# Stick-breaking attention without weights: running products applied to differences of neighbouring values, and wide weight splits moved to VectorE

## The chip, the cores and the metric

The kernel runs on one core of a Trainium2 chip. The metric is the device time of one execution in microseconds (us), as the median of several runs. The engines are named as the profile names them: PE is TensorE (PEld its weight loads), DVE is VectorE, ACT is ScalarE, POOL is GpSimd, and SP is SyncE, which issues the DMAs.

## What is computed

Two decoder layers over 1024 tokens of width 1024, all in float32. Each layer projects x with w_in, runs three token mixers side by side (4 heads of stick-breaking attention, 4 of latent attention with a softmax, called MLA, and 8 of RWKV-7), applies w_o and a layer norm, then a gated feed-forward network with a second layer norm. The part that is changed is stick-breaking attention, per block of 128 queries:

```python
z = jnp.einsum('bhqd,bhkd->bhqk', qb, k).astype(jnp.float32) * scale
past = kpos[None, :] < qpos[:, None]
log_keep = jnp.where(past, jax.nn.log_sigmoid(-z), 0.0)
log_later = lax.cumsum(log_keep, axis=3, reverse=True) - log_keep
w = jnp.where(past, jnp.exp(jax.nn.log_sigmoid(z) + log_later), 0.0)
return jnp.einsum('bhqk,bhkd->bhqd', w.astype(v.dtype), v)
```

With keep = sigmoid(-z), a key's weight is (1 - keep) times the product of the keeps of all later keys. So the weight of key j is R(j+1) - R(j), where R(j) is the running product of the keeps from j to the end.

## The kernel before

One layer is written as four stages: phase A (the projections, the preparation of RWKV, its triangular inverse `rw_inv` and its recurrent chain), attention (MLA and stick-breaking interleaved), the output projection, and the feed-forward network. In the first layer phase A lies at about 20 to 545 us of the profile, attention at 545 to 737, and the feed-forward network runs to 1555. The second layer repeats this.

Every matrix product works on a float32 operand split in two, hi and lo, with three products per tile. `split` (lines 197 to 199) makes them: ScalarE casts hi, and then another engine subtracts it from the source to get lo. For a weight tile of 128x1024 that engine is an argument: VectorE, or GpSimd where `eng` says so. `wload` (line 230) loads a weight tile by one SyncE DMA into `raw` and splits it into `whi` and `wlo`, two buffers each. GpSimd takes the subtraction in `proj_sb`, in `proj_rw` for the feature tiles 1 to 3 of phase A, and for four of the eight tiles of w_o (`w0l`, and `wol` with k of 2 and 5). That is 38 splits in the two layers: 30 of `wlo`, four of `w0l` and four of `wol`.

Attention runs as two generators per mixer (`hp` 0 and 1, for the two heads of a pair), and each yields a block of queries at a time. A stick block (`stick_block`, `stick_post`) takes a score tile from PE, applies tanh(z/2) on ScalarE into `mexp` (three buffers), masks the diagonal square with an affine select on GpSimd (line 393), and then runs three steps on VectorE: keep = 0.5 - 0.5 tanh of the keys shifted by one into `kp`, one of the three buffers LA, T and pd (line 394); the running product from the end (line 396); and the weight, (1 + tanh) times the running product (line 397). PE transposes the weights (`w_transpose`, line 336), ScalarE copies them out, and once both heads of the pair are there `av_store` multiplies them with V. Blocks of pair 0 go from 1 to 8 tiles of keys, blocks of pair 1 from 8 to 1, so there are 64 stick blocks in the two layers.

Where each instruction stands in its engine's queue is decided by the framework's scheduler from its own estimates and the priorities in `PRIORITY`; every engine then runs its queue strictly in that order. A change in one instruction's engine can therefore move others.

Of the kernel before, what the change touches and what calls it, by code (L numbers as in the profile page):

```python
# [12 lines left out]
ALU = mybir.AluOpType  # L13
# [4 lines left out]
P = 128  # L18
S = 1024
# [3 lines left out]
NT = S // P  # L23
IN_COLS = 2912
SBQ, SBK, SBV = 0, 256, 512
# [44 lines left out]
class Body:  # L70
    def __init__(self, ctx, tc, a):
        self.ctx, self.tc, self.nc, self.a = ctx, tc, tc.nc, a
        self.n = 0
        self.ptags = {}
        self.rot = 0
        self.sq = 0
        self.sn = self.kn = 0
        self.pairs = {}

    def nm(self, s):  # L80
# [180 lines left out]
    def proj_sb(self, l, pool, step):  # L261
        nc, W = self.nc, self.a["w_in"][l]
        for j in range(2):
            for base, dst in ((SBQ, self.sqd), (SBK, self.skd)):
                hi, lo = self.wload(W, [(base + j * P, P)], nc.gpsimd)
                d = self.t(pool, [P, S], "pst", bufs=4)
                self.proj_copy(hi, lo, d)
                nc.sync.dma_start(dst[j], d)
                step(4)
        for j in range(2):  # L270
            hi, lo = self.wload(W, [(SBV + j * P, P)], nc.gpsimd)
            d = self.t(pool, [P, S], "pst", bufs=4)
            self.proj_copy(hi, lo, d)
            o = self.t(pool, [P, S], "pst", bufs=4)
            for q in range(2):
                pt = self.ps2()
                for i in range(4):
                    ii = 4 * q + i
                    nc.tensor.transpose(pt[:, i * P : i * P + P], d[:, ii * P : ii * P + P], self.ident)
                nc.vector.tensor_copy(o[:, q * 512 : q * 512 + 512], pt)  # L280
            step(4)
            nc.sync.dma_start(self.svd[j], o.rearrange("p (i v) -> p i v", v=P))
# [29 lines left out]
        for a, b in zip(ms, ms[1:]):  # L312
            self.tc.add_manual_dep(b.ins, a.ins.name, mybir.DependencyInfo(mybir.DependencyClass.NoSync, mybir.DependencyReason.DATA), reason="array halves take turns")

    def attn_out(self, wts, nb, V, av):
        ms = []
        for j in range(nb):
            for hp in range(2):
                hc = slice(hp * 64, hp * 64 + 64)
                ms.append(self.nc.tensor.matmul(av[hc], V[:, j, hc], wts[hp][:, j, :], start=j == 0, stop=j == nb - 1))  # L320
        self.in_order(ms)

    def pieces(self, LL):
# [16 lines left out]
    def stick(self, wp, ip, hp):  # L340
        for pr in range(2):
            if hp == 0:
                self.sv = self.t(wp, [P, NT, P], "mv")
                self.nc.sync.dma_start(self.sv, self.svd[pr])
            V = self.sv
            qk = self.stick_qk(wp, pr, hp)
            for i in range(NT)[:: 1 - 2 * pr]:
                self.stick_block(i, pr, hp, qk, V, wp, ip)
                yield

    def stick_qk(self, wp, pr, hp):
        nc = self.nc
# [19 lines left out]
    def stick_block(self, i, pr, hp, qk, V, wp, ip):  # L372
        nc = self.nc
        mm = nc.tensor.matmul
        q2, k2, kl = qk
        nb, LL = i + 1, (i + 1) * P
        qs = slice(i * P, i * P + P)
        be = self.t(wp, [P, S], "mexp", bufs=3)
        n = self.sn = self.sn + 1
        self.kn += 1  # L380
        kp = self.kp3[self.kn % 3]
        for u, (a0, a1) in enumerate(self.pieces(LL)):
            self.sq = 1 - self.sq
            s = self.pst(("py", "pq")[self.sq])[:, : a1 - a0]
            mm(s, q2[:, qs], k2[:, a0:a1], start=True, stop=False)
            mm(s, q2[:, qs], kl[:, a0:a1], start=False, stop=True)
            nc.scalar.activation(be[:, a0:a1], s, AF.Tanh, scale=0.0625)
        self.stick_post(be, kp, i, LL, nb, n, V, hp, pr, wp)

    def stick_post(self, be, kp, i, LL, nb, n, V, hp, pr, wp):  # L390
        nc = self.nc
        dg = be[:, i * P : LL]
        nc.gpsimd.affine_select(out=dg, in_=dg, pattern=[[-1, P]], base=0, channel_multiplier=1, compare_op=ALU.is_gt, fill=-1.0)  # L393
        nc.vector.tensor_scalar(kp[:, : LL - 1], be[:, 1:LL], -0.5, 0.5, op0=ALU.mult, op1=ALU.add)
        kv = kp[:, : LL - 1][:, ::-1]
        nc.vector.tensor_tensor_scan(kv, kv, self.ones.to_broadcast([P, LL - 1]), 1.0, op0=ALU.mult, op1=ALU.mult)
        nc.vector.scalar_tensor_tensor(be[:, :LL], be[:, :LL], 1.0, kp[:, :LL], op0=ALU.add, op1=ALU.mult)  # L397
        wt = self.w_transpose(self.wt4[:, n % 6], be, nb, "pa")
        self.pair(("s", pr, i), wt, hp, nb, V, self.mixd[pr], i, wp, "pa", 0.5)

    def pair(self, key, wt, hp, *args):
        if key in self.pairs:
# [4 lines left out]
            self.pairs[key] = wt  # L407

    @prioritized
    def av_store(self, wts, nb, V, dst, i, wp, tag, sc):  # L410
        nc = self.nc
        av = self.pst(tag)[:, :P]
        self.attn_out(wts, nb, V, av)
        ot = self.t(wp, [P, P], "avo", bufs=2)
        nc.scalar.mul(ot, av, sc)
        nc.sync.dma_start(dst[:, i * P : i * P + P], ot)

    def exact2(self, ps, st, src, tp, rows=slice(0, P)):
# [146 lines left out]
    def mla_post(self, st, e, pcs, n, nb, sc, pr, hp, i, V, wp):  # L565
        nc = self.nc
        if n == 1:
            nc.vector.reciprocal(st[:, 6:7], st[:, 4:5])
        else:
            nc.scalar.activation(st[:, 7:8], st[:, 0:1], AF.Exp, scale=sc, bias=st[:, 3:4])  # L570
            nc.vector.scalar_tensor_tensor(st[:, 5:6], st[:, 4:5], st[:, 7:8], st[:, 5:6], op0=ALU.mult, op1=ALU.add)
            nc.vector.reciprocal(st[:, 6:7], st[:, 5:6])
        for u, (a0, a1) in enumerate(pcs):
            if u < n - 1:
                nc.vector.tensor_scalar(e[:, a0:a1], e[:, a0:a1], st[:, 7:8], st[:, 6:7], op0=ALU.mult, op1=ALU.mult)
            else:
                nc.vector.tensor_scalar(e[:, a0:a1], e[:, a0:a1], st[:, 6:7], None, op0=ALU.mult)
        self.sn += 1
        wt = self.w_transpose(self.wt4[:, self.sn % 6], e, nb)
        self.pair(("m", pr, i), wt, hp, nb, V, self.mixd[2 + pr], i, wp, "av", 1.0)  # L580

    def q2(self, tp):
        return self.t(tp, [P, W2], "q2", bufs=self.q2n)
# [351 lines left out]
    def oproj(self, l, wr, nxt, side, cm, other, xsrc, co, cx):  # L935
        nc, a = self.nc, self.a
        with cm:
# [8 lines left out]
            for k in range(2, KT):  # L946
                if k >= len(wr):
                    wr.append(self.wo_load(l, k))
                self.split(*wos[k], wr[k], nc.gpsimd if k % 3 == 2 else None)
            co.close()  # L950
            self.new_xT(self.pool(cx, "xT", side=other))
            zs = []
# [112 lines left out]
    def phase_a(self, l, side, other, lp, co, cc):  # L1065
# [32 lines left out]
                    next(inv, None)  # L1098

        for ft in range(4):  # L1100
            eng = nc.gpsimd if ft else None
            k = self.proj_rw(l, 4 + ft, pp, "pst", eng)
            step(6)
            prep = self.rw_prep(ft, k, w2a2, tp)
            r = self.proj_rw(l, ft, pp, "pst", eng)
            step(6)
            v = self.proj_rw(l, 8 + ft, pp, "pst", eng)
            step(99)
            u = (0, 2, 4, 2)[ft]
            for hf in range(2):  # L1110
                self.rw_stage1(ft, hf, [r, k, v], prep, A6[:, u : u + 2], tp)
            if ft % 2:
                inv = self.rw_inv(ft // 2, ip, A6[:, 2 * (ft // 2) : 2 * (ft // 2) + 4])
# [22 lines left out]
    def run(self):  # L1136
# [28 lines left out]
        for l in range(L):  # L1165
# [15 lines left out]
            with ExitStack() as c:  # L1181
                self.psum(c, sc=(512, 2), av=(512, 2))
                aw = self.pool(c, "attn", bufs=2, side=side)
                ms = [self.mla(aw, hp) for hp in range(2)]
                self.wt4 = self.t(self.ip, [P, 6, NT, P], "Aa")
                self.kp3 = [self.t(self.ip, [P, S], n) for n in ("LA", "T", "pd")]
                for t in self.kp3:
                    nc.gpsimd.memset(t, 0.0)
                for t in range(MLA_AHEAD):
                    next(ms[t % 2])  # L1190
                cc.close()
                self.w0h = self.t(self.wq, [P, 2, D], "w0h", F32R)
                self.w0l = self.t(self.wq, [P, 2, D], "w0l", F32R)
                aw3 = self.pool(c, "attn3", bufs=2, side=other)
                st = [self.stick(aw3, self.ip, hp) for hp in range(2)]
                seq = sorted([(t + o, n, g) for n, (g, o) in enumerate(zip((ms[0], st[0], ms[1], st[1]), STREAM_ORDER)) for t in range(17)], key=lambda x: x[:2])
                for _, _, g in seq:
                    next(g, None)
                nxt = self.mix_load(NT - 1)
                wr = [self.wo_load(l, k) for k in range(6)]  # L1200
                for k in range(2):
                    self.split(self.w0h[:, k], self.w0l[:, k], wr[k], nc.gpsimd)
            cp.close()
            with ExitStack() as c:
                self.psum(c, ps=(512, 2), mt=(512, 2))
# [42 lines left out]
```

## Time and profile before

| what | us |
|---|---|
| three runs | 3115.67, 3118.68, 3125.54 (median 3118.68) |
| the profiled execution's own time | 3115.81 |
| its span, first to last instruction | 3114.1 |
| PE busy in the span | 2955.1 (95%) |
| DVE, ACT, POOL busy | 1790.4, 1043.3, 328.5 |

The profile is of one execution. Its time is 2.9 us below the median of the three runs, and 1.7 us of it lie outside the span. A busy PE is not a PE at its peak: its clock is granted in steps (PEclk, the share of full speed), and at half clock the same matmul takes twice as long and still counts as busy. `<-` in a row of groups separates what is written from what is read; in a row of waits it names what ended the wait.

### The profile page before, as it was taken

How to read it: one execution, taken by the hardware profiler on the slowest of the kernel's cores; microseconds unless marked ns; L12 is line 12 of the kernel's file. 1: busy time of each engine (PE TensorE's matmuls, PEld its weight loads, DVE VectorE, ACT ScalarE, POOL GpSimd, SP SyncE). 2: the span in 40 equal slices, each digit the busy share in tenths (PEclk: the TensorE clock that was granted, in tenths of full speed). 3: DMA queues.
4: the chain of work that ended last, by engine and by line, in shares of the span. 5: the costliest groups of instructions: out<-in, count | busy, mean ns of one | idle time of the engine just before them, and what ended most of it. 6: DMA issues, size and time to landing. Idle time of an engine off the chain costs nothing. (4 is left out here: it accounts for less than half of the span.)

```text
span 3114.1 us, 41891 instructions
## 1 busy us (share of the span) xinstructions
PE 2955.1 (95%) x16572; PEld 2339.9 (75%) x16572; DVE 1790.4 (57%) x2842; ACT 1043.3 (34%) x1801; POOL 328.5 (11%) x346
## 2 busy tenths in 40 slices
PE   8998999888999999999999888999899999999998
PEld 6666777666888888888876667776678888888887
DVE  4569673886644444444645687658865443444436
ACT  5443443763222112221244443447622111212120
POOL 0111231132000000000001121320410000000000
PEclk9998999999999999999999999999999999999999
DMA  4343656413421111111124446563234111111111
GB/s 131 98 143 87 197 176 194 120 52 123 168 68 55 48 41 48 55 48 55 61 81 117 119 114 196 171 203 93 86 126 162 54 41 41 48 55 48 54 48 55
DMA packets 338260, 301.78 MB, mean 97 GB/s; under 512 B 24200, under 2 KB 302992, under 8 KB 338064
## 3 DMA queue, kind: packets, MB, share of 16 engines
q1 hardware_dynamic: 338064, 299.11, 32.4%
q8 instruction: 131, 2.15, 0.3%
q14 instruction: 65, 0.53, 0.1%
HBM read 208.87 MB, written 90.18 MB: 96 GB/s over the span
## 5 line engine op out<-in xcount | busy, mean ns | idle before, releaser
L203 PE MATMUL psmm<-xTh,whi 128*128 128x512 f32 x2144 | 858.3, 400 | 0.0
L204 PE MATMUL psmm<-xTl,whi 128*128 128x512 f32 x2144 | 856.6, 400 | 0.0
L205 PE MATMUL psmm<-xTh,wlo 128*128 128x512 f32 x2144 | 854.2, 398 | 0.0
L198 ACT CAST whi<-raw 128x1024 fp32r<-128x1024 f32 x152 | 159.9, 1052 | 1108.4 <-PE psmm L204 1100.7
L203 PEld LDWEIGHTS psmm<-xTh,whi 128*128 128x128 f32 x2144 | 406.2, 189 | 94.4 <-issue 5.3
L204 PEld LDWEIGHTS psmm<-xTl,whi 128*128 128x128 f32 x2144 | 406.0, 189 | 93.5 <-issue 3.9
L205 PEld LDWEIGHTS psmm<-xTh,wlo 128*128 128x128 f32 x2144 | 405.7, 189 | 93.5 <-issue 4.4
L199 DVE TENSOR_TENSOR wlo<-raw,whi 128x1024 fp32r<-128x1024 f32 x122 | 148.9, 1220 | 430.2 <-ACT whi L198 422.6
L1050 DVE TENSOR_TENSOR y<-y,psps 128x512 f32<-128x512 f32 x288 | 196.4, 687 | 171.7 <-PE psps L205 171.4
L203 PE MATMUL psps<-wdh,hh 128*128 128x512 f32 x672 | 267.0, 397 | 0.0
L204 PE MATMUL psps<-wdl,hh 128*128 128x512 f32 x672 | 263.1, 392 | 0.0
L205 PE MATMUL psps<-wdh,hl 128*128 128x512 f32 x672 | 260.3, 392 | 0.0
L913 POOL TENSOR_TENSOR lrs<-lrs,mhalf 128x1 f32<-128x1 f32 x32 | 29.3, 914 | 1650.4 <-DVE lrs L912 1650.4
L203 PEld LDWEIGHTS psps<-wdh,hh 128*128 128x128 f32 x672 | 126.1, 188 | 36.4 <-ACT hh L198 5.5
L205 PEld LDWEIGHTS psps<-wdh,hl 128*128 128x128 f32 x672 | 126.2, 188 | 27.1
L204 PEld LDWEIGHTS psps<-wdl,hh 128*128 128x128 f32 x672 | 126.3, 188 | 25.8
L1025 DVE TENSOR_TENSOR cv<-cv,psmm 128x1024 f32<-128x1024 f32 x44 | 53.7, 1221 | 142.8 <-PE psmm L205 137.9
L199 DVE TENSOR_TENSOR wdl<-raw,wdh 128x1024 fp32r<-128x1024 f32 x42 | 51.4, 1225 | 89.0 <-ACT wdh L198 89.0
L199 POOL TENSOR_TENSOR wlo<-raw,whi 128x1024 fp32r<-128x1024 f32 x30 | 74.8, 2494 | 194.7 <-ACT whi L198 178.3
L839 PE MATMUL pspa<-RBl,PSl 128*128 128x128 f32 x512 | 71.5, 287 | 17.7 <-ACT QC L842 9.3
L1020 ACT ACTIVATE cv<-cv 128x1024 f32<-128x1024 f32 x44 | 46.7, 1061 | 115.8 <-DVE cv L1019 115.8
L839 PEld LDWEIGHTS pspa<-RBl,PSl 128*128 128x128 f32 x512 | 64.9, 197 | 25.2 <-ACT QC L842 11.2
(444 smaller groups left out, 4696.0 us busy)
## 6 DMA issues: line engine op xcount, KB each, us to landing
raw<-in_ffn_w_up_dram SPq DMA_DIRECT2D x88, 512.0 KB
raw<-in_w_in_dram SPq DMA_DIRECT2D x44, 512.0 KB
raw<-in_ffn_w_down_dram SPq DMA_DIRECT2D x44, 512.0 KB
rbd<-RB SPq DMA_DIRECT2D x64, 256.0 KB
PSl<-psd SPq DMA_DIRECT2D x32, 512.0 KB
RBl<-rbd SPq DMA_DIRECT2D x32, 512.0 KB
psd<-Vz SPq DMA_DIRECT2D x64, 128.0 KB
xxd<-X SPq DMA_DIRECT2D x64, 128.0 KB
```

The source lines that it names most:

```text
L198: self.nc.scalar.copy(hi, src)
L199: (eng or self.nc.vector).tensor_tensor(lo, src, hi.bitcast(F32), op=ALU.subtract)
L203: mm(out, lh, rh, start=start, stop=False)
L204: mm(out, lh, rl, start=False, stop=False)
L205: mm(out, ll, rh, start=False, stop=stop)
L839: nc.tensor.matmul(pQ[:, f, e, :], PSh[:, f, h, e, :], RBh[:, f, h, e, :], start=True, stop=True)
L913: nc.gpsimd.tensor_tensor(rs, rs, self.mhalf[:, 0:1], op=ALU.pow)
L1020: nc.scalar.activation(cv, cv, AF.Gelu)
L1025: nc.vector.tensor_tensor(cv, cv, pg, op=ALU.mult)
L1050: nc.vector.tensor_tensor(y[:, i, hs], y[:, i, hs], ps, op=ALU.add)
```

## The change

Two things are changed. First, stick-breaking attention no longer forms weights. By summation by parts, the sum of (R(j+1) - R(j)) V(j) over the keys equals the sum of R(j) (V(j-1) - V(j)) plus a last term. So the running products themselves are transposed and multiplied with differences of neighbouring rows of V. A new function `stick_steps` makes these differences once for each pair of heads: two more loads from `svd` (V shifted by one row), a memset, a 128x1024 subtraction on GpSimd, a 128x1024 copy on ScalarE, and a DMA of one row into the copy, which stands for the tile on the diagonal (`Vd`). The select, the affine step and the running product stay; they now work in place in `mexp`, and the step that multiplied (1 + tanh) into the product, line 397 before, is gone. So are the three buffers `kp3` and their memsets; LA, T and pd hold the differences instead. Second, the 38 wide weight splits that GpSimd did are done by VectorE.

```diff
-                hi, lo = self.wload(W, [(base + j * P, P)], nc.gpsimd)
+                hi, lo = self.wload(W, [(base + j * P, P)])
...
-            hi, lo = self.wload(W, [(SBV + j * P, P)], nc.gpsimd)
+            hi, lo = self.wload(W, [(SBV + j * P, P)])
...
-                ms.append(self.nc.tensor.matmul(av[hc], V[:, j, hc], wts[hp][:, j, :], start=j == 0, stop=j == nb - 1))
+                ms.append(self.nc.tensor.matmul(av[hc], (Vd if j == nb - 1 else V)[:, j, hc], wts[hp][:, j, :], start=j == 0, stop=j == nb - 1))
...
-                self.sv = self.t(wp, [P, NT, P], "mv")
-                self.nc.sync.dma_start(self.sv, self.svd[pr])
+                self.sv = self.stick_steps(wp, pr)
...
+    def stick_steps(self, wp, pr):
+        nc = self.nc
+        V, U = (self.t(wp, [P, NT, P], "mv") for _ in range(2))
+        nc.gpsimd.memset(U[0:1, 0, :], 0.0)
+        nc.sync.dma_start(V, self.svd[pr])
+        nc.sync.dma_start(U[1:P], self.svd[pr][0 : P - 1])
+        nc.sync.dma_start(U[0:1, 1:NT, :], self.svd[pr][P - 1 : P, 0 : NT - 1, :])
+        r3 = lambda t: t.rearrange("p (j v) -> p j v", v=P)
+        if pr:
+            dv, dd = r3(self.t(self.ip, [P, S], "pd")), self.t(wp, [P, NT, P], "mdd", bufs=1)
+        else:
+            dv, dd = (r3(self.t(self.ip, [P, S], n)) for n in ("LA", "T"))
+        nc.gpsimd.tensor_tensor(dv, U, V, op=ALU.subtract)
+        nc.scalar.copy(dd, dv)
+        nc.sync.dma_start(dd[P - 1 : P], self.svd[pr][P - 2 : P - 1])
+        return dv, dd
...
-        nc.vector.tensor_scalar(kp[:, : LL - 1], be[:, 1:LL], -0.5, 0.5, op0=ALU.mult, op1=ALU.add)
-        kv = kp[:, : LL - 1][:, ::-1]
-        nc.vector.tensor_tensor_scan(kv, kv, self.ones.to_broadcast([P, LL - 1]), 1.0, op0=ALU.mult, op1=ALU.mult)
-        nc.vector.scalar_tensor_tensor(be[:, :LL], be[:, :LL], 1.0, kp[:, :LL], op0=ALU.add, op1=ALU.mult)
+        nc.vector.tensor_scalar(be[:, :LL], be[:, :LL], -0.5, 0.5, op0=ALU.mult, op1=ALU.add)
+        kv = be[:, :LL][:, ::-1]
+        nc.vector.tensor_tensor_scan(kv, kv, self.ones.to_broadcast([P, LL]), 1.0, op0=ALU.mult, op1=ALU.mult)
...
-                self.split(*wos[k], wr[k], nc.gpsimd if k % 3 == 2 else None)
+                self.split(*wos[k], wr[k])
...
-            eng = nc.gpsimd if ft else None
+            eng = None
...
-                self.kp3 = [self.t(self.ip, [P, S], n) for n in ("LA", "T", "pd")]
-                for t in self.kp3:
-                    nc.gpsimd.memset(t, 0.0)
...
-                    self.split(self.w0h[:, k], self.w0l[:, k], wr[k], nc.gpsimd)
+                    self.split(self.w0h[:, k], self.w0l[:, k], wr[k])
```

The scheduler's order changes with it, and three places bear on the prediction. The first is VectorE near the end of attention in the first layer, where the last stick blocks of pair 1 run. Before (a scan is printed as SCALAR_TENSOR_TENSOR with `ones`; line 394 is the affine step, line 397 the weight):

```order
L394 TENSOR_SCALAR LA_4945<-mexp_6737 128x639
L396 SCALAR_TENSOR_TENSOR LA_4945<-LA_4945,ones_90 128x639
L394 TENSOR_SCALAR T_4946<-mexp_6775 128x511
L397 SCALAR_TENSOR_TENSOR mexp_6737<-mexp_6737,LA_4945 128x640
L396 SCALAR_TENSOR_TENSOR T_4946<-T_4946,ones_90 128x511
L394 TENSOR_SCALAR pd_4947<-mexp_6792 128x511
L397 SCALAR_TENSOR_TENSOR mexp_6775<-mexp_6775,T_4946 128x512
L396 SCALAR_TENSOR_TENSOR pd_4947<-pd_4947,ones_90 128x511
L394 TENSOR_SCALAR LA_4945<-mexp_6821 128x383
L397 SCALAR_TENSOR_TENSOR mexp_6792<-mexp_6792,pd_4947 128x512
L396 SCALAR_TENSOR_TENSOR LA_4945<-LA_4945,ones_90 128x383
L397 SCALAR_TENSOR_TENSOR mexp_6821<-mexp_6821,LA_4945 128x384
```

After, the same place (line 408 is the affine step, line 410 the scan):

```order
L408 TENSOR_SCALAR mexp_6763<-mexp_6763 128x512
L408 TENSOR_SCALAR mexp_6779<-mexp_6779 128x512
L410 SCALAR_TENSOR_TENSOR mexp_6763<-mexp_6763,ones_90 128x512
L410 SCALAR_TENSOR_TENSOR mexp_6779<-mexp_6779,ones_90 128x512
L408 TENSOR_SCALAR mexp_6807<-mexp_6807 128x384
L410 SCALAR_TENSOR_TENSOR mexp_6807<-mexp_6807,ones_90 128x384
L199 TENSOR_TENSOR wol_6954<-pst_6925,woh_6953 128x1024
L408 TENSOR_SCALAR mexp_6822<-mexp_6822 128x384
L410 SCALAR_TENSOR_TENSOR mexp_6822<-mexp_6822,ones_90 128x384
L408 TENSOR_SCALAR mexp_6847<-mexp_6847 128x256
L410 SCALAR_TENSOR_TENSOR mexp_6847<-mexp_6847,ones_90 128x256
```

The weights have left the queue, and a split of w_o stands where two scans and a weight stood.

The second place is VectorE in phase A of the first layer, in the preparation of feature tile 1: line 653 (666 after) is the last product of one half, lines 684 and 685 (697 and 698 after) mask what PE made of it, and lines 305 and 308 finish a projection. Before:

```order
L653 TENSOR_TENSOR q_325_1763<-pspa_1756,pst_1546 128x512
L684 TENSOR_TENSOR Aa_877<-pspq_1782,maskA_94 128x256
L685 TENSOR_TENSOR RB_1766<-pspq_1782,maskA_94 128x4x64
L684 TENSOR_TENSOR Aa_877<-pspa_1783,maskA_94 128x256
L685 TENSOR_TENSOR RB_1766<-pspa_1783,maskA_94 128x4x64
```

After:

```order
L666 TENSOR_TENSOR q_325_1763<-pspa_1756,pst_1546 128x512
L199 TENSOR_TENSOR wlo_2083<-raw_2081,whi_2082 128x1024
L305 TENSOR_TENSOR pst_1866<-pst_1866,shc_1867 128x1
L308 SCALAR_TENSOR_TENSOR pst_1866<-psmm_1896,pv_66_286,pst_1866 128x511
L697 TENSOR_TENSOR Aa_877<-pspq_1782,maskA_94 128x256
L698 TENSOR_TENSOR RB_1766<-pspq_1782,maskA_94 128x4x64
```

A weight split and the end of a projection now stand ahead of the two masks.

The third place is GpSimd where stick-breaking begins in the first layer (L899, 912 after, belongs to the RWKV chain; L393, 407 after, is the affine select of a stick block). Before:

```order
L899 TENSOR_TENSOR mo_4909<-mo_4909,bvl_4753 128x256
L899 TENSOR_TENSOR mo_4922<-mo_4922,bvl_4821 128x256
L393 AFFINE_SELECT mexp_5199<-mexp_5199 128x128
L393 AFFINE_SELECT mexp_5271<-mexp_5271 128x128
L393 AFFINE_SELECT mexp_5323<-mexp_5323 128x128
```

After:

```order
L912 TENSOR_TENSOR mo_4909<-mo_4909,bvl_4753 128x256
L912 TENSOR_TENSOR mo_4922<-mo_4922,bvl_4821 128x256
L353 MEMSET mv_5179 1x128
L362 TENSOR_TENSOR LA_5184<-mv_5179,mv_5178 128x1024
L407 AFFINE_SELECT mexp_5202<-mexp_5202 128x128
L353 MEMSET mv_6301 1x128
L407 AFFINE_SELECT mexp_5273<-mexp_5273 128x128
```

The subtraction of `stick_steps`, which waits for its loads, stands ahead of the first select.

## Rows read from the trace of the kernel before

**Rows 1.** Page of the profile, part 1: busy time, share, instructions.

```profile
PE 2955.1 (95%) x16572; PEld 2339.9 (75%) x16572; DVE 1790.4 (57%) x2842; ACT 1043.3 (34%) x1801; POOL 328.5 (11%) x346
```

**Rows 2.** Stretches: us, PE, PEld, DVE, ACT, POOL busy (count), PEclk, DMA share, GB/s.

```profile
590.00:640.00 50.00, 46.88 (x403) 36.31 (x404) 45.45 (x104) 39.02 (x105) 3.04 (x7) 1.00 0.22 55
640.00:695.00 55.00, 46.45 (x372) 36.89 (x368) 48.81 (x72) 35.32 (x85) 22.99 (x25) 0.94 0.22 68
695.00:735.00 40.00, 31.24 (x208) 22.13 (x204) 35.26 (x50) 22.67 (x52) 18.35 (x15) 0.87 0.30 92
2235.00:2275.00 40.00, 32.01 (x211) 23.00 (x208) 35.50 (x50) 23.07 (x55) 17.20 (x15) 0.87 0.31 91
100.00:300.00 200.00, 177.75 (x1107) 133.04 (x1105) 152.10 (x246) 89.27 (x161) 39.77 (x31) 0.95 0.41 113
```

**Rows 3.** Waits of PE, 695 to 735: total, times, longest.

```profile
PE pspa L336 <- DVE mexp L397: 6.9, 6, 3.0
PE psmm L204 <- POOL wol L199: 1.8, 1, 1.8
```

**Rows 4.** Waits of PE, 2235 to 2275; that for GpSimd as before.

```profile
PE pspa L336 <- DVE mexp L397: 6.0, 5, 3.0
```

**Rows 5.** Timeline of VectorE, 695 to 745: start, us, instruction, idle before.

```profile
694.28 0.96 DVE L397 SCALAR_TENSOR_TENSOR mexp<-mexp,LA 128x768 f32<-128x768 f32 x1
699.53 3.10 DVE L397 SCALAR_TENSOR_TENSOR mexp<-mexp,T 128x768 f32<-128x768 f32 x1
...
723.46 2.86 DVE L396 TENSOR_TENSOR_SCAN pd<-pd,ones 128x255 f32<-128x255 f32 x1
...
728.15 0.69 DVE L396 TENSOR_TENSOR_SCAN LA<-LA,ones 128x255 f32<-128x255 f32 x1
...
731.18 0.28 DVE L397 SCALAR_TENSOR_TENSOR mexp<-mexp,T 128x128 f32<-128x128 f32 x1
```

**Rows 6.** Timeline of GpSimd in that stretch.

```profile
699.15 2.66 POOL L199 TENSOR_TENSOR w0l<-raw,w0h 128x1024 fp32r<-128x1024 f32 x1 [3.04 <-ACT w0h L198]
723.24 2.53 POOL L199 TENSOR_TENSOR wol<-pst,woh 128x1024 fp32r<-128x1024 f32 x1 [1.57 <-ACT woh L198]
```

**Rows 7.** Waits of PE, 590 to 695.

```profile
PE psav L336 <- DVE mexp L575: 5.0, 5, 2.7
PE pspa L336 <- DVE mst L561: 2.4, 1, 2.4
```

**Rows 8.** Timeline of VectorE, 184 to 200.

```profile
192.50 2.90 DVE L648 TENSOR_TENSOR q<-ta,q 128x256 f32<-128x256 f32 x2
```

**Rows 9.** Timeline of GpSimd, 184 to 200.

```profile
192.75 2.37 POOL L199 TENSOR_TENSOR wlo<-raw,whi 128x1024 fp32r<-128x1024 f32 x1 [4.13 <-ACT whi L198]
```

**Rows 10.** Timeline of PE, 190 to 199.

```profile
195.46 1.11 PE L671 MATMUL pspq<-ident,q 128*128 128x128 f32 x4 [4.29 <-DVE q L648]
```

**Rows 11.** Line 648: ns min/median/max, first and last start.

```profile
L648 DVE TENSOR_TENSOR q<-ta,q x32: 404/424/2566, 145.8 to 1899.1; 128x256 f32<-128x256 f32 x32
```

**Rows 12.** Groups of the whole trace: busy, mean ns, idle before.

```profile
L199 DVE TENSOR_TENSOR wlo<-raw,whi 128x1024 fp32r<-128x1024 f32 x122 | 148.9, 1220 | 430.2 <-ACT whi L198 422.6 <-DMA y<-x1d 7.6
L305 DVE TENSOR_TENSOR pst<-pst,shc 128x1 f32<-128x1 f32 x26 | 21.5, 828 | 16.7 <-ACT pst L303 16.7
L397 DVE SCALAR_TENSOR_TENSOR mexp<-mexp,T 128x128 f32<-128x128 f32 (+7 forms) x22 | 21.5, 979 | 0.1
L199 POOL TENSOR_TENSOR wlo<-raw,whi 128x1024 fp32r<-128x1024 f32 x30 | 74.8, 2494 | 194.7 <-ACT whi L198 178.3 <-issue 15.7 <-DMA psd<-T 0.6
```

**Rows 13.** Waits of VectorE, 20 to 545.

```profile
DVE wlo L199 <- ACT whi L198: 24.2, 5, 8.6
```

**Rows 14.** Timelines of SyncE and GpSimd where the first stick block begins.

```profile
569.21 0.33 SPq L344 DMA_DIRECT2D mv<-svd  x1
...
575.60 1.22 POOL L393 TENSOR_SCALAR_AFFINE_SELECT mexp<-mexp 128x128 f32<-128x128 f32 x1 [9.99 <-ACT mexp L387]
```

More of the change, by code (lines that the diff above doesn't have):

```diff
@@ L76, in __init__ @@
         self.sq = 0
-        self.sn = self.kn = 0
+        self.sn = 0
         self.pairs = {}
@@ L313, in in_order, with attn_out @@
             self.tc.add_manual_dep(b.ins, a.ins.name, mybir.DependencyInfo(mybir.DependencyClass.NoSync, mybir.DependencyReason.DATA), reason="array halves take turns")
-    def attn_out(self, wts, nb, V, av):
+    def attn_out(self, wts, nb, V, Vd, av):
         ms = []
@@ L379, in stick_block @@
         n = self.sn = self.sn + 1
-        self.kn += 1
-        kp = self.kp3[self.kn % 3]
         for u, (a0, a1) in enumerate(self.pieces(LL)):
@@ L387, in stick_block, with stick_post @@
             nc.scalar.activation(be[:, a0:a1], s, AF.Tanh, scale=0.0625)
-        self.stick_post(be, kp, i, LL, nb, n, V, hp, pr, wp)
-    def stick_post(self, be, kp, i, LL, nb, n, V, hp, pr, wp):
+        self.stick_post(be, i, LL, nb, n, V, hp, pr, wp)
+    def stick_post(self, be, i, LL, nb, n, V, hp, pr, wp):
         nc = self.nc
@@ L393, in stick_post @@
         nc.gpsimd.affine_select(out=dg, in_=dg, pattern=[[-1, P]], base=0, channel_multiplier=1, compare_op=ALU.is_gt, fill=-1.0)
-        nc.vector.tensor_scalar(kp[:, : LL - 1], be[:, 1:LL], -0.5, 0.5, op0=ALU.mult, op1=ALU.add)
-        kv = kp[:, : LL - 1][:, ::-1]
-        nc.vector.tensor_tensor_scan(kv, kv, self.ones.to_broadcast([P, LL - 1]), 1.0, op0=ALU.mult, op1=ALU.mult)
-        nc.vector.scalar_tensor_tensor(be[:, :LL], be[:, :LL], 1.0, kp[:, :LL], op0=ALU.add, op1=ALU.mult)
+        nc.vector.tensor_scalar(be[:, :LL], be[:, :LL], -0.5, 0.5, op0=ALU.mult, op1=ALU.add)
+        kv = be[:, :LL][:, ::-1]
+        nc.vector.tensor_tensor_scan(kv, kv, self.ones.to_broadcast([P, LL]), 1.0, op0=ALU.mult, op1=ALU.mult)
         wt = self.w_transpose(self.wt4[:, n % 6], be, nb, "pa")
-        self.pair(("s", pr, i), wt, hp, nb, V, self.mixd[pr], i, wp, "pa", 0.5)
+        self.pair(("s", pr, i), wt, hp, nb, *V, self.mixd[pr], i, wp, "pa")
     def pair(self, key, wt, hp, *args):
@@ L409, in av_store @@
     @prioritized
-    def av_store(self, wts, nb, V, dst, i, wp, tag, sc):
+    def av_store(self, wts, nb, V, Vd, dst, i, wp, tag):
         nc = self.nc
         av = self.pst(tag)[:, :P]
-        self.attn_out(wts, nb, V, av)
+        self.attn_out(wts, nb, V, Vd, av)
         ot = self.t(wp, [P, P], "avo", bufs=2)
-        nc.scalar.mul(ot, av, sc)
+        nc.scalar.copy(ot, av)
         nc.sync.dma_start(dst[:, i * P : i * P + P], ot)
@@ L579, in mla_post @@
         wt = self.w_transpose(self.wt4[:, self.sn % 6], e, nb)
-        self.pair(("m", pr, i), wt, hp, nb, V, self.mixd[2 + pr], i, wp, "av", 1.0)
+        self.pair(("m", pr, i), wt, hp, nb, V, V, self.mixd[2 + pr], i, wp, "av")
     def q2(self, tp):
```

## The prediction

> **What bounds the kernel now.** I read the page's busy times first, then the stretches of the attention stage, then who PE waits for in them, and last the instructions that it waits for. PE is busy for 95% of the span [rows 1], so a change can only give back PE's idle time, the time that it spends at half clock, or PE work, and no PE work is removed here. In the feed-forward network PE has no idle time that this change touches. What is left is attention and phase A.
>
> In the middle of attention PE is busy 46.9 us of 50 and then 46.5 of 55, and VectorE 45.5 and 48.8 in the same stretches [rows 2]: the two run nearly level. In the last 40 us of attention PE falls to 31.2 (32.0 in the second layer) with the clock at 0.87, while VectorE stays at 35.3 and 35.5 [rows 2]. There PE waits for line 397, the weights that the change removes, 6.9 us in six waits, and 1.8 us for a split of w_o on GpSimd [rows 3]; the second layer shows 6.0 [rows 4] and the same 1.8. So the end of attention is VectorE's, and the middle is shared. In phase A VectorE is busy 152 us of 200 and the clock stands at 0.95 [rows 2].
>
> A second thing is to be seen in these rows. Some VectorE instructions take two to four times as long as others of their kind: a weight of 128x768 takes 3.10 us and another 0.96, a scan of 128x255 takes 2.86 us and another 0.69 [rows 5]. The long ones began at 699.53 and 723.46, within half a microsecond of a GpSimd subtraction of a weight tile of w_o, at 699.15 for 2.66 us and at 723.24 for 2.53 [rows 6]. In phase A the same happens: two of line 648, which take 0.42 us each as a rule [rows 11], took 2.90 together from 192.50 [rows 8], over a split on GpSimd that ran from 192.75 for 2.37 [rows 9], and PE stood still for 4.29 us until they were done [rows 10]. So a split on GpSimd is not free for VectorE.
>
> **The change part by part.** The sum is made against the profiled execution, 3115.8 us.
>
> *The end of attention.* The weights leave VectorE's queue. Twelve of them stand in the last 40 us, from 0.96 us down to 0.28 [rows 5], 7.7 us in sum without the long one's excess. With them and the splits on GpSimd go two excesses, 2.1 (3.10 less 0.96) and 2.2 (2.86 less 0.69). Four splits come in at 1.22 each [rows 12], 4.9 us. VectorE's queue is 7.1 us shorter, against 8.7 and 7.8 us of PE's waits. PE is then next to be late with its own transposes and the chain of one block, so not all of it comes back. Between nothing and 16.5 us I take 6 a layer: **-12**.
>
> *The clock there.* 13% of 40 us is 5.2 us lost a layer [rows 2]. PE's clock falls in stretches where it has just waited. If three quarters of the waits go, some of the low stretches go. Between nothing and 10.4 I take half: **-5**.
>
> *The middle.* From 590 to 695 PE waits 5.0 us for the softmax's scaling, line 575, and 2.4 for its line 561 [rows 7]. Neither is touched, but both stand in VectorE's queue behind weights and scans, and some 0.8 to 1.2 us of weight leaves for each block (the group's mean is 0.98 [rows 12]). Between nothing and 14.8 for the two layers I take half: **-7**. The clock of 0.94 costs 3.3 us in 55 [rows 2]; I take 1 a layer: **-2**.
>
> *The splits of phase A.* Thirty `wlo` splits leave GpSimd, 2.49 us each, and cost VectorE 1.22 each [rows 12], 36.6 us in all. Against that stand the excesses, bounded from both sides. The smallest instruction of the stage, line 305 on 128x1, has a mean of 828 ns over 26 [rows 12] though there is hardly any work in it; at 0.16 us apiece its excess alone is 17 us, or 0.6 for each split. The pair at 192.50 lost 2.06. So a split that moves changes VectorE's time by something between +0.6 and -0.8 us. I take zero for the load and count only the wait that the rows show: at 192.50 PE waited on the excess itself, so 2 us, and the second layer repeats the stage: **-4**. The clock of 0.95 over 200 us costs 10 us a layer [rows 2]; I take 1.5 of it: **-3**.
>
> On this point the Trainium skill speaks against the change. "Perfetto Trace Analysis", section "Optimizing Scalar/DVE Operations", says that work may be moved off a saturated VectorE, to ScalarE or even to GpSimd, and adds that the port which those two share may undo it. By its first half the 36.6 us would be pure loss, and these two terms would be a plus; by the rows above they are -7. Which half holds decides a rival below.
>
> *What is added.* Each pair of heads gets a subtraction on GpSimd of the shape of a split, 2.5 us [rows 12], a ScalarE copy, a memset and three more DMAs. In the first layer the subtraction stands ahead of the first select. Its load of V is issued at 569.21 as before, the first select started 6.4 us later, at 575.60 [rows 14], and it must now wait for two loads and the subtraction. Behind it wait the affine step, the scan and the first transposes of stick-breaking; PE has MLA's matmuls to run meanwhile. Between nothing and 2.5 us plus a late load I take 1.5 a layer: **+3**. The second subtraction may hold VectorE up by 2.1, like a split; the weights that have left (a block's mean of 0.98 us, several blocks) cover it, and without that cover it costs 2 a layer. The copies fall into attention, where ScalarE is busy 39 us of 50 [rows 2], and are hidden by its remaining 11. The memsets and the buffers `kp3` go, for nothing, since GpSimd idles there.
>
> Sum: 3115.8 - 12 - 5 - 7 - 2 - 4 - 3 + 3 = 3085.8, so **3086**. The profiled execution lies 2.9 below the median of the runs, well inside the range.
>
> **The rivals.**
>
> *PE has it all, and little comes back.* The waits on VectorE are only the places where a saturated PE shows its seams; without them the next wait is the chain of a block. For it: PE is busy 94% in the middle [rows 2]. Against it: at the end VectorE is busier than PE. Then only the two longest waits at the end that GpSimd caused go, 3.0 and 1.8 a layer [rows 3, 4], less 3 for the start: 3115.8 - 9.6 + 3 = 3109.
>
> *A split waits at the head of VectorE's queue (slower).* GpSimd could stand idle until ScalarE had cast the tile; VectorE can't. The order shows such a place: the split right behind line 653, ahead of the masks on which PE waits. Of the splits that VectorE does in phase A already, five waited for the cast, 24.2 us, so 4.8 each, the longest 8.6 [rows 13]. If a third of the fifteen of a layer do that with PE behind them, it costs 24 a layer, 48 in all: 3086 + 48 = 3134. The gain is gone when the thirty splits cost PE 1.0 us each, and the kernel is measurably slower from 1.4. Against it: the scheduler placed each split by its own estimate of the cast.
>
> *VectorE becomes the bound of phase A.* No excess comes back, 18.3 us a layer are added, and PE sees them in the share in which VectorE is busy, 0.76: 14 a layer. Then 3115.8 - 26 + 3 + 28 = 3121. This is what the first half of the rule in "Perfetto Trace Analysis" (Trainium skill) would make of it. Against it stand [rows 6, 8, 9].
>
> *More comes back.* PE's waits in attention vanish with their clock: 16.5 + 10.4 + 14.8 + 6.6 = 48, and phase A gives 10: 3058.
>
> **How the numbers follow.** This kernel can tell about 0.3%, 9.4 us, from no change: faster is below 3109, slower above 3128. Forecast (3068 to 3102) 0.50; more comes back 0.15; little comes back 0.15, half of it below 3109; VectorE the bound 0.09; a split at the head of the queue 0.11. Faster 0.50 + 0.15 + 0.07 = 0.72, same 0.08 + 0.09 = 0.17, slower 0.11. The range from 3056 to 3114 leaves out the last two rivals; the forecast's own range is 3068 to 3102.
>
> **What would show it.** Right, if at the end of either attention stage VectorE is busy for some 28 us where it was 35, PE waits there under 4 us, and no VectorE instruction of that stretch takes over 2.5 us; if no line 305 takes over 1 us except over a GpSimd product of phase A; and if line 648 no longer holds PE for 4.3 us. The rival of the waiting split shows as VectorE waits for the cast of `whi` in phase A well above 24 us with PE idle behind them. The prediction is wrong if phase A grows by more than attention shrinks, or if the first transposes of stick-breaking hold PE for over 5 us.

## The result, and the profile after

The changed kernel takes 3139.04 us (median of six runs, 3134.55 to 3144.98) against 3118.11 for the kernel before beside it: a ratio of 1.0069, 95% interval 1.0051 to 1.0087. It is slower; the forecast was 3086, faster.

The stages show that two changes of opposite sign lie in this. Each row below is one stage: phase A of the first layer, attention of the first layer, attention of the second, cut at the first score matmul of MLA and at the last copy of attention's output. Columns: the stretch, its length, each engine's busy time with its instructions, the clock, the DMA share and rate. First the kernel before, then the changed one:

```profile
core 0: us, PE busy (x) PEld busy (x) DVE busy (x) ACT busy (x) POOL busy (x), PEclk, DMA share, GB/s
0.00:546.30 546.30, 497.82 (x3465) 380.65 (x3466) 343.05 (x633) 237.41 (x423) 99.81 (x105) 0.97 0.50 147
546.30:737.10 190.80, 163.74 (x1233) 124.45 (x1232) 163.91 (x323) 128.03 (x326) 52.14 (x58) 0.93 0.30 87
2088.60:2276.70 188.10, 162.12 (x1233) 123.53 (x1232) 163.30 (x323) 127.43 (x326) 49.28 (x58) 0.94 0.32 89
```

```profile
0.00:533.50 533.50, 500.49 (x3466) 384.87 (x3466) 337.93 (x649) 237.54 (x423) 62.09 (x87) 0.97 0.52 150
533.50:750.80 217.30, 158.05 (x1231) 122.67 (x1232) 140.86 (x295) 128.59 (x327) 44.78 (x58) 0.86 0.28 79
2086.00:2300.00 214.00, 160.54 (x1233) 125.66 (x1232) 139.03 (x295) 128.68 (x327) 45.96 (x58) 0.86 0.28 81
```

Phase A is 12.8 us shorter. Attention is 26.5 and 25.9 us longer, although VectorE has 23 us less to do there and PE does the same matmuls. PE stands idle 59 us of the stage where it stood 27, and the clock is 0.86 instead of 0.93.

The waits of all engines in the first 107 us of attention say where (who waited for whom: total, times, longest):

```profile
POOL LA L362 <- DMA mv<-svd: 26.7, 1, 26.7
PE pspy L399 <- ACT mexp L401: 21.8, 2, 20.8
DVE mexp L408 <- POOL mexp L407: 21.2, 4, 20.0
ACT T L363 <- POOL LA L362: 20.5, 1, 20.5
...
PE pssc L203 <- ACT mexp L575: 18.8, 4, 17.3
...
ACT mdd L363 <- POOL pd L362: 16.9, 1, 16.9
POOL pd L362 <- DMA mv<-svd: 16.3, 1, 16.3
```

Read it from the DMA outward. Line 355, `U[1:P] <- svd[0 : P - 1]`, loads V shifted by one row. GpSimd's subtraction (line 362) waits 26.7 us for it, and 16.3 us for the second pair of heads. Behind the subtraction stand the selects (line 407), for which VectorE's affine step waits 20.0 us; ScalarE's copy (line 363) waits 20.5 us at the head of its queue, with the tanh (line 401) and the exponentials of the softmax (line 575) behind it. PE stops for those two, 20.8 us and 17.3 us.

How the load runs while PE stands is in two windows of the changed kernel:

```profile
562.00:568.00 6.00, 3.18 (x17) 2.21 (x17) 3.81 (x6) 3.18 (x7) 0.00 (x0) 0.87 0.06 27
577.00:582.00 5.00, 0.00 (x0) 0.00 (x0) 0.00 (x0) 0.00 (x0) 0.00 (x0) 0.50 0.06 26
```

26 GB/s and a DMA share of 0.06, one sixteenth: one DMA engine carries the 508 KB (127 rows of 4 KB) alone. At 26 GB/s that is 20 us. In the second window nothing else in the core works.

The signs named for the other steps came out as follows. The end of attention (last 41 us of the first layer, where [rows 2, 3] have 40; its window, then PE's waits there) answers to [rows 2, 3]:

```profile
710.00:751.00 41.00, 36.83 (x272) 26.48 (x272) 32.66 (x53) 28.97 (x72) 6.89 (x12) 0.96 0.37 111
```

```profile
PE pspa L336 <- DVE mst L574: 1.6, 2, 1.1
PE psav L336 <- DVE mexp L590: 1.2, 2, 0.9
PE pspa L336 <- ACT avo L428: 0.8, 1, 0.8
PE pspa L336 <- DVE mexp L410: 0.5, 1, 0.5
```

PE waits 4.1 us instead of 8.7 (the sign was under 4) and is busy 36.8 instead of 31.2. The one-column line 305 and line 661 (648 before) answer to [rows 11, 12] (shortest, median, longest in ns):

```profile
L305 DVE TENSOR_TENSOR pst<-pst,shc x26: 133/153/631, 75.7 to 1886.8; 128x1 f32<-128x1 f32 x26
```

```profile
L661 DVE TENSOR_TENSOR q<-ta,q x32: 371/422/465, 145.5 to 1896.7; 128x256 f32<-128x256 f32 x32
```

The long ones of both are gone: the mean of line 305 was 828 ns, and the longest of line 648 2566.

### The profile page after: what moved, and what is told of

The parts are those of the page before. It is cut to its first block, busy times and chain, and to the rows that moved or that the text cites. A ratio compares the mean times of both kernels' runs of the same rounds, so it can differ in the third digit from the quotient of the medians.

```text
span 3140.8 us, 41790 instructions
## 1 busy us (share of the span) xinstructions
PE 2952.9 (94%) x16572; PEld 2345.2 (75%) x16572; DVE 1733.3 (55%) x2816; ACT 1045.2 (33%) x1805; POOL 242.5 (8%) x310
## 4 chain that ended last, share of the span: by engine, by line
PE 75%; DVE 8%; issue 8%; DMA 4%; ACT 3%; POOL 2%; SPq 0%; POOLq 0%; DVEq 0%; ACTq 0%
PE psmm L203 16%; PE psmm L204 16%; PE psmm L205 16%; PE psps L203 5%; PE psps L205 5%; PE psps L204 5%; DMA mv<-svd 2%; PE pspa L852 1%; DVE pd L737 1%; PE pspi L796 1%; PE psmt L214 1%; DVE LA L733 1%; DVE Aa L775 1%; PE pspa L692 1%; DVE T L738 0%
## 5 line engine op out<-in xcount | busy, mean ns | idle before, releaser
L199 DVE TENSOR_TENSOR wlo<-raw,whi 128x1024 fp32r<-128x1024 f32 x152 | 185.5, 1221 | 465.3 <-ACT whi L198 456.0
L410 DVE TENSOR_TENSOR_SCAN mexp<-mexp,ones 128x128 f32<-128x128 f32 (+7 forms) x64 | 87.8, 1379 | 0.6
L852 PE MATMUL pspa<-RBl,PSl 128*128 128x128 f32 x512 | 73.6, 291 | 13.4 <-ACT QC L855 8.8
```

Source lines behind the costliest of these rows:

```text
L199: (eng or self.nc.vector).tensor_tensor(lo, src, hi.bitcast(F32), op=ALU.subtract)
L852: nc.tensor.matmul(pQ[:, f, e, :], PSh[:, f, h, e, :], RBh[:, f, h, e, :], start=True, stop=True)
```

## The experiments

Main theory: the loss is the one load of 127 rows, which one DMA engine carries; all the rest is a gain, phase A's more than forecast. Rivals: the added subtraction, copy and queue order cost it however fast the load is; or splits in VectorE's queue cost it. In the table "before" is the kernel before that ran beside each one, and the last three columns are the stages of the profiled execution, cut as above.

| kernel | us | before | ratio (95%) | phase A | att. 1 | att. 2 |
|---|---|---|---|---|---|---|
| before | 3118.1 | | | 546.3 | 190.8 | 188.1 |
| changed | 3139.0 | 3118.1 | 1.0069 (1.0051-1.0087) | 533.5 | 217.3 | 214.0 |
| 1 load 112+15 | 3068.2 | 3112.4 | 0.9856 (0.9840-0.9871) | 532.8 | 177.4 | 179.4 |
| 2 load 124+3 | 3071.4 | 3112.4 | 0.9866 (0.9846-0.9886) | 528.5 | 177.8 | 179.9 |
| 3 splits only | 3074.6 | 3112.4 | 0.9874 (0.9857-0.9891) | 533.5 | 182.3 | 183.9 |
| 4 parts only, 127 rows | 3173.9 | 3112.4 | 1.0193 (1.0177-1.0208) | 545.0 | 222.3 | 216.1 |
| 5 parts only, 112+15 | 3103.3 | 3113.3 | 0.9969 (0.9959-0.9979) | 548.4 | 184.2 | 183.7 |
| 6 unread load, one tile | 3153.3 | 3113.3 | 1.0126 (1.0111-1.0141) | 544.3 | 211.6 | 207.5 |
| 7 nothing added | 3063.9 | 3113.3 | 0.9842 (0.9827-0.9856) | 534.3 | 177.5 | 172.4 |
| 8 GpSimd dummies | 3144.9 | 3113.3 | 1.0101 (1.0086-1.0116) | 532.7 | 213.0 | 208.1 |
| 9 unread, ScalarE's queue | 3156.2 | 3110.6 | 1.0138 (1.0109-1.0167) | 541.4 | 212.8 | 208.5 |
| 10 changed, ScalarE's queue | 3150.4 | 3110.6 | 1.0120 (1.0098-1.0142) | 535.2 | 225.5 | 213.4 |
| 11 subtract on VectorE | 3068.3 | 3110.6 | 0.9855 (0.9829-0.9882) | 530.9 | 176.3 | 183.2 |
| 12 and no GpSimd products | 3048.9 | 3110.6 | 0.9800 (0.9776-0.9824) | 523.9 | 172.4 | 176.6 |
| 13 unread, two tiles, SP | 3156.0 | 3117.0 | 1.0117 (1.0101-1.0134) | 544.5 | 199.7 | 196.8 |
| 14 unread, two tiles, ScalarE | 3124.7 | 3117.0 | 1.0025 (1.0014-1.0037) | 547.5 | 184.0 | 184.3 |
| 15 copy on GpSimd | 3126.0 | 3117.0 | 1.0026 (1.0015-1.0037) | 529.5 | 220.0 | 199.7 |

**1 and 2. The rows of the load.** The changed kernel, with one line edited (the second has 124 in the place of 112):

```diff
-        nc.sync.dma_start(U[1:P], self.svd[pr][0 : P - 1])
+        nc.sync.dma_start(U[1 : 112 + 1], self.svd[pr][0:112])
+        nc.sync.dma_start(U[112 + 1 : P], self.svd[pr][112 : P - 1])
```

> The changed kernel with the shifted load U[1:128] in two: 112 rows and 15 rows. Theory A (the load of 127 rows of 4 KB goes through one of the sixteen DMA engines, 20 us twice a layer, and holds the subtraction, the selects behind it and so PE): the wait of the subtraction falls from 26.7 and 16.3 us to some 6 and under 3, PE's two long stops of 20.9 and 17.3 us in the first layer's attention go, attention falls from 217 us to 185 to 195 a layer, and the time from 3139 to about 3085 (3065 to 3100). Theory B (the work added, a subtraction on GpSimd and a copy on ScalarE ahead of the first select, and the new order of the queues cost it, whatever the load takes): the stops shrink by a few us at most, the time stays above 3125.

> The same with the shifted load in 124 rows and 3 rows, a smaller dose. Theory A, by the Trainium skill, 'DMA: Bandwidth & Descriptors', section on why a DMA increments its semaphore by 16: the engines are the largest count up to sixteen that divides the rows, so 124 rows go through four and take a quarter of the 20 us, an estimate of 5 us. Then the time lies at or a little above that of the split into 112 and 15, by at most 10 us. If the cost comes from the count of rows in another way (an odd first row, a load that is not whole), 124 rows are as slow as 127 and the time stays at 3130 to 3140. Theory B: as for 112 and 15, above 3125.

Both come out at the fast end: the same bytes in the same tile, and 0.0213 of the time is gone, 66 us. Windows while the long piece of the second pair's load runs, of 112 rows (issued at 576.09 behind V's load, so its rows come last) and then of 124:

```profile
578.00:578.50 0.50, 0.50 (x5) 0.31 (x6) 0.50 (x2) 0.31 (x2) 0.00 (x0) 1.00 1.02 401
```

```profile
579.00:581.00 2.00, 2.00 (x28) 1.70 (x24) 2.00 (x6) 1.47 (x5) 0.00 (x0) 1.00 0.25 95
```

All sixteen engines for 112 rows (share 1.02), a share of 0.25, four, for 124, where 127 rows had 0.06. All three loads begin at the second row of the tile, so that odd start is not the cause. The Trainium skill, "DMA: Bandwidth & Descriptors", section "Why a DMA increments its semaphore by 16 and not by 1", states the rule: the engines are the largest number up to sixteen that divides the rows, and it names 127 as a case of one. The trace agrees at all three sizes. That four engines cost no more time than sixteen (the intervals overlap) suggests that a load of some 5 us still fits into the slack ahead of the first select.

**3, 4 and 5. The change in halves.** The splits alone in the kernel before (`eng` dropped at the five places of the diff), summation by parts alone with its 127 rows, and the same with 112 and 15.

> The kernel before with nothing but the 38 wide splits moved from GpSimd to VectorE. Theory A: phase A gives back what it gave in the changed kernel, 12.8 and some 15 us, and the end of attention a few us; the time is 3080 to 3098 against 3118. Rival C (VectorE's longer queue costs as much as GpSimd's splits did, as the forecast's phase A rivals had it): 3110 to 3135.

> The changed kernel with the 38 splits put back on GpSimd: summation by parts alone, with its load of 127 rows. Theory A: attention loses what it lost in the changed kernel, 26 us a layer, or a few more by the splits at its end, and phase A is as before; the time is 3160 to 3180. Rival D (the loss in attention comes from splits that now stand in VectorE's queue, not from the load): attention is back near 190 us and the time is at or below 3118.

> Summation by parts alone (the 38 splits back on GpSimd), with the shifted load in 112 and 15 rows. If the load of 127 rows was the whole loss of summation by parts, this is a gain: phase A as before, attention 5 to 10 us a layer shorter than before, 3092 to 3108 against 3112. If summation by parts costs more than it gives even with a quick load (the added subtraction, copy and queue order), it is at or above the kernel before.

By the ratios the splits give 39 us by themselves, all of phase A's gain and 8.5 and 4.2 us of attention. Summation by parts gives 10 us with a quick load and costs 60 us with the slow one; the difference, 0.0224 or 70 us, is the load again. So no half holds a loss but that line, and the rivals of the splits are out.

**6, 9, 13 and 14. The load without a reader.** In the kernel before, one more load that nobody reads; 6 on SP's queue, 9 on ScalarE's. 13 and 14 repeat both with two tiles of 3.5 KB a row (13's edit; 14 has `nc.scalar` in it):

```diff
                 self.nc.sync.dma_start(self.sv, self.svd[pr])
+                self.nc.sync.dma_start(self.t(wp, [P, 7, P], "u", bufs=2)[1:P], self.svd[pr][0 : P - 1, 0:7])
```

> The kernel before with one more load of 127 rows a pair of heads, into a tile that nobody reads. If the loss comes from those who wait for the load (the subtraction, the selects and the copy behind it), the time stays within 10 us of before, although the load still takes 20 us. If the transfer itself is what hurts (the queue that it fills, the loads of queries and keys behind it), attention grows by 10 us a layer or more and the time by over 20.

> The load of 127 rows that nobody reads, in the kernel before, now issued by ScalarE on its own queue instead of SP's. On SP's queue it cost 40 us: PE stood 19.9 us for a ScalarE copy that waited 22.1 us for an earlier store of attention's output, which had been issued behind the load. If that is the order within one queue (whatever follows the load there must pass the engine that it fills), the store now lands in time, PE's stop of 19.9 us goes and the time is within 10 us of before. If the busy engine itself is what the store waits for, on any queue, the stop stays and the time is again 30 us or more above before.

> The unread load again on SP's queue, of 127 rows of 3.5 KB, now into two tiles, so that the second load needn't wait for the first (that wait, 8.1 us on SP and 22.9 us on ScalarE, was a fault of the two runs with one tile). If the order within a queue is what costs, stores of attention's output that are issued behind the loads land late and PE stands some 15 to 20 us a layer for the copy that needs their tile: 3130 to 3150. If the cost of the two runs before came from the wait for the one tile, the time is within 10 us of before.

> The same two loads, issued by ScalarE on its own queue. If the order within a queue is what costs, SP's stores no longer stand behind the load: within 10 us of before. If a busy engine delays every transfer on every queue alike, it is as slow as on SP's queue.

By the main theory an unread load is free, and it cost 39 us. The first two runs don't say why: with one tile the second load must wait for the first, which held SP 8.1 us and ScalarE 22.8 us. With two tiles the queue shows. ScalarE's copy of attention's output waits for an earlier store of the same buffer, and PE for the copy; from 590 to 640, first on SP's queue, then on ScalarE's:

```profile
ACT avo L416 <- DMA mixd<-avo: 17.3, 1, 17.3
...
PE pspa L336 <- ACT avo L416: 15.2, 1, 15.2
```

```profile
ACT avo L416 <- DMA mixd<-avo: 2.7, 1, 2.7
```

A store of 64 KB that is issued behind the load on the same queue waits until that one engine has worked off its rows; from another queue it doesn't. Attention is 15.7 and 12.5 us shorter for it. The Trainium skill, "DMA: Bandwidth & Descriptors", section "Queues, rings and completion order", says that SP and ScalarE each own a ring on each engine and that a ring is worked off in order; these two runs agree. Both runs also lose 8 to 12 us a layer behind attention, in the projection by w_o, where no such load runs. Part of that is work that has moved: in the kernel before 24 matmuls of w_o start inside the attention of the first layer, in 13 and 14 six, and behind it PE now waits 6.3 us for splits of w_o. So part of 14's shorter attention (184.0 us against 190.8) is the other side of that loss. How the two extra tiles move w_o, and why 14 is still 8 us above before in sum, was not settled.

**10 and 15. The load with its readers.** The changed kernel with its 127 rows on ScalarE's queue (`nc.scalar.dma_start`), and with the copy moved (`nc.gpsimd.tensor_copy(dd, dv)`).

> The changed kernel with its load of 127 rows issued by ScalarE on its own queue. If the loss of the changed kernel is that of its readers (subtraction, selects, ScalarE's copy wait 20 us whatever the queue), it stays slow: 3115 to 3140 against 3139. If it is that of the transfers queued behind the load, it comes near the version with 112 and 15 rows: 3070 to 3095.

> The changed kernel, load of 127 rows and all, with the copy of the differences on GpSimd instead of ScalarE, so that nothing waits for the load at the head of ScalarE's queue. If ScalarE's wait is what stops PE (PE's two stops ended with ScalarE's exponentials of the softmax, which need no part of the load), PE goes on with MLA and the time falls from 3139 to 3115 or less. If VectorE's affine step, which waits for the select behind the subtraction, holds VectorE's queue and PE just as well, the time stays at 3125 to 3145.

On another queue nothing is won: the subtraction still waits 26.5 us and ScalarE's copy 23.1 us. In the changed kernel the readers alone are enough for the loss. (Why 10 is above the changed kernel, 1.0120 against 1.0069, stays open.) With the copy on GpSimd 0.0043 comes back, 13 us, nearly all in the second layer. In the first, VectorE takes ScalarE's place:

```profile
DVE mexp L408 <- POOL mexp L407: 45.5, 9, 19.3
...
POOL LA L362 <- DMA mv<-svd: 25.6, 1, 25.6
...
PE pspa L336 <- DVE mst L585: 20.6, 1, 20.6
```

The affine step waits for the select and holds MLA's softmax behind it. That is the second outcome that I had written down, at its edge (3126 us, of 3125 to 3145): the readers stop PE through both queues, and to free one is not enough.

**7. What is added, once the load is quick.** `stick_steps` returns `V, V` right after the load of V, so the differences are left out and the kernel computes something else.

> The kernel with the load in 112 and 15 rows, without what summation by parts adds: no shifted load, no subtraction, no copy, no patches of rows; the products weigh the values themselves, so this leaves out the differences, and its output is not the reference's. Beside the first run it prices what is added once the load is quick. The forecast's price was 3 us in all: then 3062 to 3070. If the subtraction, the copy and their waits cost more than thought, 3040 to 3058.

0.9842 against 0.9856 with everything in, 4 us, and the intervals overlap: the price of 3 us for subtraction, copy and patches was about right.

**8. A GpSimd subtraction and VectorE.** Behind each select of the version with 112 and 15 rows:

```diff
+        z = V[0][:, 0:7]
+        nc.gpsimd.tensor_tensor(self.t(wp, [P, 7, P], "scr", bufs=1), z, z, op=ALU.subtract)
```

> The kernel with the load in 112 and 15 rows, and behind each of the 64 selects of stick-breaking one GpSimd subtraction of 128x896 (about 2.1 us) into a tile that nobody reads. No work of VectorE is added or moved. If a GpSimd subtraction of two tiles holds VectorE (the Trainium skill, 'SBUF — State Buffer', section on who interferes with whom, has such a lock), VectorE instructions of attention that begin under it take up to 2 us longer, 15 to 40 us in sum, and the time grows by 15 to 60 us. If the long VectorE instructions of the trace before had another cause, the time grows by less than 8 us.

It costs 0.0245, 76 us, more than expected. VectorE has no new work, and its busy time in the attention of the first layer goes from 142.4 to 173.1 us. One group of the softmax as an example, without the dummies and with them:

```profile
L589 DVE TENSOR_SCALAR mexp<-mexp,mst 128x512 f32<-128x512 f32 x12 | 8.3, 694 | 0.3
```

```profile
L591 DVE TENSOR_SCALAR mexp<-mexp,mst 128x512 f32<-128x512 f32 x12 | 12.3, 1025 | 0.3
```

The Trainium skill, "SBUF — State Buffer", section "Who interferes with whom", says that a VectorE instruction in a two-port mode and a GpSimd instruction take one shared pair of ports in turn, each for its whole length. The traces agree: the dummies, 1.74 us each at the median, lengthen what VectorE does beside them, by 0.96 us a dummy in that stage. Not every instruction is lengthened: the row maxima of 128x512 that VectorE reads from PE's output (20 TENSOR_REDUCE) take 679 ns in the mean with the dummies and 684 without. The selects do queue behind the dummies on GpSimd, which is busy 60 us more a layer, but VectorE's waits for a select hardly grow, from 13.2 us in the attention of the first layer to 13.9.

**11 and 12. Less on GpSimd.** From the version with 112 and 15 rows, the subtraction on VectorE; then also line 653's products and the splits of q and k (`SPLIT_STICK = (0, 0)`).

> The version with the load in 112 and 15 rows, its four subtractions on VectorE instead of GpSimd. By the last run a GpSimd subtraction of two tiles holds VectorE for about its own time; the subtraction is 2.4 us there and about 1.2 on VectorE. Expected: 0 to 6 us less than the version with 112 and 15 rows, 3061 to 3068. If VectorE's queue at that point is what PE waits for, 0 to 4 us more.

> The same, and the 32 products and 32 splits of q and k that are left on GpSimd (128x256 and 64x256) on VectorE too. Their excess on VectorE was 14 us in sum, and at a third of a microsecond each they cost VectorE about 21 us there. If what matters is that VectorE's work is not held up at a bad moment, as with the 38 splits, the time falls by another 5 to 15 us; if VectorE's sum decides, it grows by 0 to 10 us.

The first changes nothing that can be measured. The second is the best version, 3048.86 us, ratio 0.9800; phase A is at 523.9 us and VectorE is busy there for 339.51 us, about as long as in run 1 (337.82), with 15 instructions more:

```profile
0.00:524.00 524.00, 492.83 (x3465) 379.14 (x3465) 339.51 (x664) 237.55 (x423) 46.56 (x71) 0.98 0.52 153
```

## Why the prediction was wrong

**What is added (+3), the step that failed.** I had written that the first select "must now wait for two loads and the subtraction" and that the cost lies between nothing and "2.5 us plus a late load". The late load then got no number, neither in the sum nor in the range, and I took the shifted load to be as quick as that of V, because it has nearly the same bytes. It takes 20 us, at a fifteenth of the rate at which 112 rows ran (26 GB/s against 401), and with it attention is 39.9 and 34.6 us longer than with 112 and 15 rows: some 66 us by the ratios, for a term of 3. The rule on rows and engines stands in the Trainium skill ("DMA: Bandwidth & Descriptors", the section named at runs 1 and 2); I had priced the load by its bytes alone. The rest of the term held (run 7). I had also named the sign, the first transposes of stick-breaking holding PE for over 5 us. What held PE, for 20.8 us, was a score matmul of stick-breaking (line 399) behind the tanh.

**Without that load the forecast would have held**: 0.9856 of the median before is 3073, inside the range from 3056 to 3114, though a gain of 45 us where 30 were forecast. Its terms would still have been off:

- *Splits of phase A (-7 with the clock).* Measured: 12.8 us in the changed kernel, and with 112 and 15 rows 13.5 in the first layer and 12.8 in the second (513.8 us from the last start of a matmul of line 204 on `wdl` in the first feed-forward network to the first score matmul, where it was 526.6), so -26. The mechanism was right, and so was the zero for VectorE's load: its busy time went from 343.05 to 337.93 with fifteen splits more, -0.34 a split, within my bounds of +0.6 and -0.8. What was mis-sized is PE's share. I counted 2 us of one wait [rows 10]; PE's idle time in the stage fell from 48.5 to 33.0 us. Two of PE's waits for VectorE in the stage, before and in the changed kernel (lines 671, 592 and 648 are 684, 605 and 661 there):

```profile
PE pspq L671 <- DVE q L648: 8.0, 2, 4.3
PE pspq L592 <- DVE q L199: 4.8, 1, 4.8
```

```profile
PE pspy L605 <- DVE q L199: 1.4, 1, 1.4
PE pspq L684 <- DVE q L661: 0.7, 1, 0.7
```

A split on GpSimd lengthens what VectorE is at, and some of that is what PE waits for next. I had priced one such wait for line 648, where there were two. From where the rest of the 15.5 us came was not taken apart.
- *End and middle of attention (-26 with the clock, +3).* Attention with 112 and 15 rows is 13.4 and 8.7 us shorter than before: -22 against -23, in part by luck, for the split between the causes was not mine: the splits alone give 8.5 and 4.2 of it, the weights that leave VectorE the rest (4.9 and 4.5). At the end VectorE was busy 32.7 us, not 28, mainly because the faster stretch holds two blocks more: a scan of 128x896 and a second one of 128x768, 2.02 and 1.75 us, with an affine step each, 5 us together. The four added splits were counted rightly (eight stand there, four of them as before). A third excess was not counted: at 715.66 an affine step of 128x383 took 2.51 us over a split on GpSimd, and another of that size 0.45.
- *The rivals.* A split at the head of VectorE's queue, and VectorE as the bound of phase A: both would have lengthened phase A, which is shorter, and run 3 rules them out. VectorE's waits for the cast did grow, from 24.2 us [rows 13] to 41.4 in phase A of the changed kernel, but without PE's idle time growing behind them. The first half of the rule in the Trainium skill, "Perfetto Trace Analysis", section "Optimizing Scalar/DVE Operations", that work may be moved off a saturated VectorE to GpSimd, would here have cost 39 us (run 3 moves it the other way; VectorE is busy for 63% of phase A before). Its second half, that the port which VectorE and GpSimd share may undo such a move, is what runs 3 and 8 show. The slower outcome came from a mechanism that stood among none of my rivals.

## What to carry to other kernels

Price every new DMA by its rows as well as its bytes, and when a load is one row short of the tile, cut it where the count divides well: 112 and 15 rows instead of 127 were worth 66 us here. Then ask what stands behind its first reader in each in-order queue, since a wait of one GpSimd subtraction stopped ScalarE and VectorE for work that needs none of the load. And a subtraction of two tiles that is moved to GpSimd to spare VectorE may spare it nothing: here 38 of them moved back gave 39 us.

## What the runs showed of the hardware that I had not expected

- A load of 127 rows ran at 26 GB/s (share 0.06), one of 124 at a share of 0.25, one of 112 at 401 GB/s (1.02).
- Such a load hurts transfers that have nothing to do with it: ScalarE waited 17.3 us for the buffer of a store issued behind it on the same queue, and 2.7 us with the load on another queue.
- 64 GpSimd subtractions that nobody reads cost 76 us; VectorE's busy time in one stage of attention grew by 31 us without new work, while its reductions of PE's output kept their 0.68 us.
